# Encoder block on one Trainium2 core: the output projection as seven half-size products, its weight sums prepared during branch A, and two attention maps joined by one multiply-add

## Chip, cores, metric

One of the eight cores of a Trainium2 chip. The metric is the device time of one execution in microseconds (us); lower is better.

## What is computed

A hybrid encoder block on 1024 tokens and 16 meta tokens, width 1024, all in float32. The part that matters here:

```python
proj = rms_norm(h) @ w_in                 # q, k, v of branches A and B, and two gates
y_a  = differential_attention(...)        # branch A: 4 heads, per head two softmax maps
#        attn = softmax(s1) - lam * softmax(s2); y = attn @ v; y = rms_norm(y) * (1 - lambda_init)
y_b  = windowed_gqa(...)                  # branch B
merged = sigmoid(ga) * (y_a @ w_ba) + sigmoid(gb) * (y_b @ w_bb)
h = h + merged @ w_o                      # the output projection, 1024 x 1024 x 1024
h = h + (silu(n @ w_gate) * (n @ w_up)) @ w_down     # n = rms_norm(h), inner width 2816
out = rms_norm(h)[:, 16:]
```

## The kernel before

Every product in this kernel keeps float32 accuracy by splitting both operands into a high half (a copy rounded to the matmul's type, made by ScalarE, "ACT") and a low half (operand minus high half, a subtraction on VectorE, "DVE", or GpSimd, "POOL"), and adding three matmuls: high x high, high x low, low x high. The helper `split` (L116 to L118) issues this pair; L117 is the ACT line, L118 the subtraction's, for all tiles.

The stages in order: the input norm and the projections for branches A and B with branch B's attention (to about 330 us); branch A, 4 heads x 8 tiles of 128 queries (330 to 608 us), into which the products that compute the two gates are filled by a list of slots; the merge (622.7 to 709.8 us), 16 products of branch B and 16 of branch A, each 12 matmuls for 128 output features and 512 tokens; the output projection (709.8 to about 801 us); the first FFN products, gate and up (to 1227 us); the down projection.

The gate products, the FFN products and the down projection are already done by the seven-product scheme of Strassen and Winograd: a product of 2 x 2 blocks with seven block products instead of eight, whose operands are sums and differences of blocks and whose results are accumulated in PSUM across products. The output projection was the one large product with eight.

**Order.** TensorE's order is written out by hand from branch A to the end (`order_pe`). The other engines and the SP queue, which issues the DMAs, are ordered by a planner that simulates the program, except for a stretch of POOL before branch A and everything in the down projection. Each engine executes its queue in order, so an instruction that waits holds all behind it.

**Branch A.** `scores_a` (L789 to L818) makes the two maps m = 1 and m = 0 of a tile: three matmul groups each, a DVE reduction with the distance bias (L805), the exponential on ACT with its row sum (L810), a reciprocal (L811). The map 1 is scaled by its reciprocal and minus lambda on POOL (L813), and DVE joins the maps (L816). TensorE's transposes of the joined map (L828) come one tile later.

```python
    nc.scalar.activation(s[m][:, 0:L], s[m][:, 0:L], AF.Exp, bias=low, scale=-1.0, accum_out=dn[:, m:m + 1])
    nc.vector.reciprocal(dn[:, m:m + 1], dn[:, m:m + 1])
    if m:
        (nc.gpsimd if t % 4 in COMBINE_POOL else nc.vector).tensor_scalar(
            s[1][:, 0:L], s[1][:, 0:L], dn[:, 1:2], neglam, ALU.mult, ALU.mult)
    yield
nc.vector.scalar_tensor_tensor(s[0][:, 0:L], s[0][:, 0:L], dn[:, 0:1], s[1][:, 0:L], ALU.mult, ALU.add)
```

`normed_a` norms the result per head; what is normed is scaled by its own mean square, `EPS` added.

**The merge.** `gated` reads a gate, applies the sigmoid and runs the 12 matmuls of `branch_mm` (L786). For branch B DVE multiplies gate and product into `tb` (L1027). For branch A DVE multiplies (L1047), POOL adds `tb` (L1048), and `split` makes the merged operand `mT` for all 1024 features and tokens. The weights are read into raw tiles (`raw_tile`, five buffers of 4 KB per partition), split by `branch_w`, `WB_BUFS` deep; gates have `GT_BUFS` = 4 buffers.

```python
order_a = [(o, h) for b in range(0, DC, 4) for h in range(2) for o in range(b, b + 4)]
for n, (o, half) in enumerate(order_a):
    if o not in ws_a:
        ws_a[o] = branch_w(ypool, o, w_ba, "a")
    gt, ps, tk = gated(1, o, half, ws_a[o], ya)
    nc.vector.tensor_tensor(gt, gt, ps, ALU.mult)
    nc.gpsimd.tensor_tensor(gt, gt, tb_row(o, tk), ALU.add)
    split(mT[:, o, 0, tk], mT[:, o, 1, tk], gt, nc.vector)
    if n >= 8:
        prep_wo(0, n - 8)
```

**The projection.** `prep_wo` reads and splits blocks of `w_o` into `op_tile` (eight buffers): 8 during the merge, 8 during the projection. `out_mm` runs 24 matmuls for each of 8 token tiles and 2 column halves (L1076), four PSUM banks at a time; `out_add` adds a bank to the residual `h2` (L1081, 16 times). `norm_f` norms a token tile (ACT square L1208, POOL L122 and L123, DVE L1210), `turn_f` transposes it and, for tiles 4 to 7, makes the sums of token halves (L1239 to L1242) for the FFN's seven products.

**The FFN's start.** `product_f` runs one of the seven products for gate (i = 0) or up (i = 1); the first twelve use only operands of products 1 and 2. Tiles 5, 6, 7 are turned before the FFN products 0, 2 and 4, each followed by `split_t`, which splits the four sums at once (DVE three lows, POOL one). `prepare` keeps weight operands ahead, at most eight tiles; it includes the weight sums on DVE (L1134 to L1140).

Of the kernel before, what the change touches and what calls it, by code (L numbers as in the profile page):

```python
# [9 lines left out]
F32 = mybir.dt.float32  # L10
# [9 lines left out]
P = 128  # L20
# [18 lines left out]
COMBINE_POOL = (0, 1, 2, 3)  # L39
# [9 lines left out]
WB_BUFS = 5  # L49
# [12 lines left out]
PAD = 96  # L62
P_BUFS = 7
S_TMP = 2
# [9 lines left out]
def encoder_block(ctx: ExitStack, tc: tile.TileContext, x, meta, norm_mix, w_in, lq1, lk1, lq2, lk2,  # L74
# [241 lines left out]
    def attend_b(g, t, qb):  # L316
# [9 lines left out]
        es = small.tile([P, 4], F32, tag="bes", name=f"bes_{nm}")  # L326
# [441 lines left out]
    apool3, close_apool3 = pool("apool3")  # L768

# [3 lines left out]

    def branch_w(p, o, src, nme, raw=None):
        if raw is None:
            raw = raw_tile(f"wbr{nme}_{o}")[:, 0:512]
            load_w(raw, o, src)
        w = raw.rearrange("p (c n) -> p c n", n=P)
        wh = p.tile([P, 2, 4, P], F32R, tag="wh", name=f"wbh{nme}_{o}", bufs=WB_BUFS)
        split(wh[:, 0], wh[:, 1], w, nc.vector if nme == "a" and o >= 4 else nc.gpsimd)  # L780
        return wh
# [6 lines left out]

    def scores_a(h, t, ld, s):  # L789
# [3 lines left out]
        mn = small.tile([P, 2, 4], F32, tag="amn", name=f"amn_{nm}")  # L793
        dn = small.tile([P, 2], F32, tag="adn", name=f"adn_{nm}")
        u0 = 896 - t * P
        for m in (1, 0):
# [13 lines left out]
            nc.scalar.activation(s[m][:, 0:L], s[m][:, 0:L], AF.Exp, bias=low, scale=-1.0, accum_out=dn[:, m:m + 1])  # L810
            nc.vector.reciprocal(dn[:, m:m + 1], dn[:, m:m + 1])  # L811
            if m:
                (nc.gpsimd if t % 4 in COMBINE_POOL else nc.vector).tensor_scalar(  # L813
                    s[1][:, 0:L], s[1][:, 0:L], dn[:, 1:2], neglam, ALU.mult, ALU.mult)
            yield
        nc.vector.scalar_tensor_tensor(s[0][:, 0:L], s[0][:, 0:L], dn[:, 0:1], s[1][:, 0:L], ALU.mult, ALU.add)  # L816
# [28 lines left out]
    def normed_a(h, c, py):  # L845
# [10 lines left out]
        nc.vector.tensor_scalar(f, pst[:, 0:4], 1.0 / P, EPS, ALU.mult, ALU.add)  # L856
# [40 lines left out]
    for n in range(AH * NT + T_LAG):  # L897
# [45 lines left out]
    order_pe.__exit__(None, None, None)  # L943
    close_apool3()
# [5 lines left out]
    tb = [ypool.tile([P, 4, S], F32, name="tb"), *yb_raw]  # L950
# [13 lines left out]
    def ps_bank(name):  # L964
        return bank(psum3, "bank", name, 8)

    pad, close_pad = pool("pad", "right")
    pad.tile([P, PAD // 4], F32, name="pad")
# [8 lines left out]
    wos = {}  # L977

    def prep_wo(q, c):
# [538 lines left out]
```

## Time and profile before

| | |
|---|---|
| median of 3 runs | 1446.95 us (1446.73 to 1448.22) |
| the profiled execution's own time | 1446.43 us |
| its span, first to last instruction | 1444.6 us |
| mean granted TensorE clock | 0.997 |
| matmuls / DVE / ACT / POOL instructions | 7279 / 1624 / 1290 / 605 |
| chain that ended last: TensorE, POOL, DVE, DMA, ACT | 80%, 6%, 5%, 3%, 2% |
| of it the output projection, PE po L1076 | 6% |

The span is what the profile's times add up to; 1.8 us of the execution lie outside it. PE is TensorE's matmuls, PEld its weight loads, which overlap; SP is the queue of the DMAs. In groups, a row has line, engine, operation, out<-in, shapes and count, then busy us and mean ns of one, then the idle time of its engine before it and what ended it. In answers on one tile or line, the three numbers behind a count are the shortest, median and longest ns of one.

### The profile page before, as it was taken

The numbers are of one execution on the slowest core, as the hardware profiler recorded it, in microseconds if no ns is written. First come the engines' busy times: TensorE is split into PE (matmuls) and PEld (weight loads), VectorE is DVE, ScalarE is ACT, GpSimd is POOL, SyncE is SP. The second block draws the span as 40 slices with busy tenths as digits, with TensorE's granted clock in tenths as the row PEclk, the third lists the DMA queues.
The fourth block names the chain that finished last, engine by engine and source line by source line (L and its number), as shares of the span: only waits on it lengthen the run. The fifth ranks groups of instructions, "written<-read, shape, count | busy, mean of one in ns | idle before, by whom it ended". The sixth has DMA issues, their size and how long they took to land.

```text
span 1444.6 us, 21159 instructions
## 1 busy us (share of the span) xinstructions
PE 1423.5 (99%) x7279; PEld 1221.1 (85%) x7279; DVE 901.6 (62%) x1624; ACT 679.5 (47%) x1290; POOL 642.6 (44%) x605
## 2 busy tenths in 40 slices
PE   8999999999999999999999999999999999999997
PEld 6988989988898989888888878888888888888886
DVE  7478536637697989624614966554555553787567
ACT  6356535545665656545413643333333333444454
POOL 5589227743333333334522665544544552000444
PEclk9999999999999999999999999999999999999999
DMA  8367668995558473586602534333332333964343
GB/s 245 87 211 231 195 160 271 283 289 208 189 168 258 147 226 126 190 255 204 224 32 88 152 103 162 110 102 110 101 103 96 110 102 102 334 205 140 124 130 139
DMA packets 188891, 242.41 MB, mean 168 GB/s; under 512 B 18208, under 2 KB 115936, under 8 KB 188784
## 3 DMA queue, kind: packets, MB, share of 16 engines
q1 hardware_dynamic: 188784, 241.07, 52.5%
q8 instruction: 57, 0.93, 0.3%
q14 instruction: 50, 0.41, 0.1%
HBM read 157.45 MB, written 77.00 MB: 162 GB/s over the span
## 4 chain that ended last, share of the span: by engine, by line
PE 80%; POOL 6%; DVE 5%; issue 4%; DMA 3%; ACT 2%; SPq 0%; POOLq 0%; DVEq 0%; ACTq 0%
PE pg L1299 27%; PE pd L1393 9%; PE pg L742 7%; PE ppa L786 6%; PE po L1076 6%; PE aps L802 3%; PE pp_qb L214 3%; PE apy L841 3%; POOL oa L118 3%; PE pp_ka L214 2%; PE pp_va L214 2%; PE apt L828 2%; PE pp_qa L214 2%; PE bpt L356 1%; PE bpy L362 1%
## 5 line engine op out<-in xcount | busy, mean ns | idle before, releaser
L118 POOL TENSOR_TENSOR wop<-wf,wop 128x512 fp32r<-128x512 f32 x128 | 173.5, 1360 | 164.7 <-ACT wop L117 150.3
L1299 PE MATMUL pg<-t,wop 128*128 128x512 f32 x1056 | 242.6, 389 | 0.0
L1299 PEld LDWEIGHTS pg<-t,wop 128*128 128x128 f32 x1056 | 198.2, 188 | 41.2
L1393 PE MATMUL pd<-ob,oa 128*128 128x512 f32 x924 | 209.9, 389 | 0.4 <-POOL oa L118 0.4
L1393 PEld LDWEIGHTS pd<-ob,oa 128*128 128x128 f32 x924 | 173.3, 188 | 36.8 <-POOL oa L118 0.9
L1299 PE MATMUL pg<-b,wop 128*128 128x512 f32 x792 | 185.6, 392 | 2.3 <-DVE c L1308 2.3
L1299 PEld LDWEIGHTS pg<-b,wop 128*128 128x128 f32 x792 | 149.4, 189 | 34.2 <-issue 2.4
L742 PE MATMUL pg<-hT_hi,gop 128*128 128x512 f32 x384 | 142.9, 397 | 0.0
L118 POOL TENSOR_TENSOR oa<-ra,oa 128x512 fp32r<-128x512 f32 x33 | 44.1, 1337 | 170.0 <-ACT oa L117 168.6
L117 ACT ACTIVATE wop<-wf 128x512 fp32r<-128x512 f32 x128 | 80.2, 631 | 83.3 <-PE pg L1299 47.8
L118 POOL TENSOR_TENSOR gop<-gr,gop 128x512 fp32r<-128x512 f32 x47 | 62.0, 1321 | 105.9 <-ACT gop L117 105.9
L117 ACT ACTIVATE oa<-ra 128x512 fp32r<-128x512 f32 x77 | 48.7, 632 | 106.1 <-PE pd L1393 46.0
L810 ACT ACTIVATE as<-as,amn 128x1040 f32<-128x1040 f32 x64 | 74.5, 1165 | 47.3 <-DVE amn L805 43.2
L1134 DVE TENSOR_TENSOR s<-wf,wf 128x512 f32<-128x512 f32 x22 | 23.7, 1077 | 107.6 <-DMA wf<-in_w_ff_gate_dram 57.4
L802 PE MATMUL aps<-ak,aq 128*128 128x392 f32 (+1 forms) x384 | 90.1, 330 | 0.7 <-DVE amn L805 0.4
L1076 PE MATMUL po<-woh,mT 128*128 128x512 f32 x384 | 88.1, 390 | 0.0
L1076 PEld LDWEIGHTS po<-woh,mT 128*128 128x128 f32 x384 | 71.9, 188 | 14.8
L742 PEld LDWEIGHTS pg<-hT_hi,gop 128*128 128x128 f32 x384 | 72.7, 189 | 11.3 <-DVE gk L747 0.2
L802 PEld LDWEIGHTS aps<-ak,aq 128*128 128x128 f32 x384 | 69.6, 189 | 14.3 <-DVE amn L805 2.0
L343 POOL TENSOR_SCALAR bs<-bs,bdn 128x432 f32<-128x432 f32 (+1 forms) x64 | 41.1, 662 | 87.1 <-DVE bdn L341 74.3
L742 PE MATMUL pg<-hT_lo,gop 128*128 128x512 f32 x192 | 76.1, 396 | 0.0
L813 POOL TENSOR_SCALAR as<-as,adn,neglam 128x1040 f32<-128x1040 f32 x32 | 39.1, 1220 | 63.9 <-DVE adn L811 44.6
(289 smaller groups left out, 3105.9 us busy)
## 6 DMA issues: line engine op xcount, KB each, us to landing
ra<-aop SPq DMA_DIRECT2D x77, 256.0 KB, 2.7
wf<-in_w_ff_gate_dram SPq DMA_DIRECT2D x24, 512.0 KB, 3.8
wf<-in_w_ff_up_dram SPq DMA_DIRECT2D x24, 512.0 KB, 3.9
aop<-as SPq DMA_DIRECT2D x44, 256.0 KB, 2.1
w_c<-in_w_in_dram SPq DMA_DIRECT2D x17, 512.0 KB, 6.1
aop<-c SPq DMA_DIRECT2D x33, 256.0 KB, 2.0
ts_d<-to SPq DMA_DIRECT2D x16, 512.0 KB, 3.4
gw<-in_w_in_dram SPq DMA_DIRECT2D x32, 256.0 KB, 4.2
```

The source lines that it names most:

```text
L117: nc.scalar.activation(hi, src, AF.Copy)
L118: lo_eng.tensor_tensor(lo, src, f32(hi), ALU.subtract)
L214: nc.tensor.matmul(ps[:, :n], a[:, c, :], b[:, c, at:at + n], start=(c == 0 and i == 0), stop=(c == DC - 1 and i == 2))
L343: nc.gpsimd.tensor_scalar(st[:, r, :W], st[:, r, :W], dn[:, r:r + 1], 1.0, ALU.mult, ALU.mult)
L742: nc.tensor.matmul(ps, op[:, a, c], quad(b, *act)[:, c], start=(p in (2, 5, 1) and c == 0 and i == 0), stop=(p in (2, 3, 4) and c == 3 and ...
L786: nc.tensor.matmul(ps, w[:, a, j, :], src(j, b, tk), start=(j == 0 and n == 0), stop=(j == 3 and n == 2))
L802: nc.tensor.matmul(ps[:, :n], qs[m][:, t * P:(t + 1) * P], ks[m][:, vv, k0:k0 + n], start=(vv == 0), stop=(vv == 1))
L810: nc.scalar.activation(s[m][:, 0:L], s[m][:, 0:L], AF.Exp, bias=low, scale=-1.0, accum_out=dn[:, m:m + 1])
L841: nc.tensor.matmul(py[:, cols], v[:kp, a, k, :], at_[:kp, k, b, :], start=(k == 0 and j == 0), stop=(k == 8))
L1076: nc.tensor.matmul(ps, mT[:, c, a, t * P:(t + 1) * P], wos[q, c][:, b], start=(c == 0 and n == 0), stop=(c == DC - 1 and n == 2))
L1299: nc.tensor.matmul(ps, op[:, x, c, :], b[:, y, c, :], start=(p in (1, 2, 5) and c == 0 and n == 0), stop=(p in (4, 2, 3) and c == 3 and n ...
L1393: nc.tensor.matmul(ps[u], oa[:, a, u * P:(u + 1) * P], ob[:, b, :], start=(p in (1, 2, 5) and j == 0 and k == 0), stop=(p in (2, 3, 4) and ...
```

## The change

1. **Output projection.** The 2 x 2 blocks of tokens (X: tokens 512 to 1023, Y: 0 to 511) and features give seven products of 512 x 512 x 512, in the order 1, 5, 6, 7, 3, 2, 4. Products 1, 6, 7 and 4 accumulate in one set of four banks, 5 and 3 in another, 2 in a third. After each, DVE adds the banks to the residual of a quarter: 28 additions.
2. **Left operands.** The differences of merged blocks (`m_sum`) and all low halves are on DVE, the high halves on ACT, issued between merge products and between row blocks of the projection. POOL's additions of `tb` are now on DVE. DVE's order is by hand from the merge of branch A to the twelfth FFN product.
3. **Right operands.** Four of the seven weight operands are sums of blocks of `w_o`. `wo_ahead` makes them in branch A, in tiles 2 to 5 of each head: reads on SP, one POOL sum, a split (ACT, POOL), a write of 512 KB to DRAM. `prep_wo` reads them back ready; the other three are read and split as before.
4. **Branch B of the merge.** All of branch A's weights are split there too, into `wba`; SP's order is by hand in this loop, and at its end the FFN's first weights and gain are read. Branch A starts with tokens 512 to 1023.
5. **Maps.** Map 1 is no longer scaled on POOL. DVE joins `s1 * f + s0` with f = minus lambda x (sum of map 0) / (sum of map 1), and map 0 is left undivided; since the result is normed, `EPS` is scaled by the square of the sum of map 0.
6. **FFN start.** Token tiles 0 to 3 are turned during product 2, tiles 4 and 5 during product 4, tiles 6 and 7 before FFN products 2 and 4. The norm's last step is issued one tile later. `split_t` splits one sum at a time by a table, lows delayed. The Silu table is loaded by a dummy activation at the end of the merge. PSUM's eight banks are two tags of four. Several tiles share buffers (`WB_BUFS` 5 to 4, copies in groups of four).

```diff
@@ scores_a @@
-            nc.scalar.activation(s[m][:, 0:L], s[m][:, 0:L], AF.Exp, bias=low, scale=-1.0, accum_out=dn[:, m:m + 1])
-            nc.vector.reciprocal(dn[:, m:m + 1], dn[:, m:m + 1])
+            nc.scalar.activation(s[m][:, 0:L], s[m][:, 0:L], AF.Exp, bias=low, scale=-1.0, accum_out=sum_of[m])
             if m:
-                (nc.gpsimd if t % 4 in COMBINE_POOL else nc.vector).tensor_scalar(
-                    s[1][:, 0:L], s[1][:, 0:L], dn[:, 1:2], neglam, ALU.mult, ALU.mult)
+                nc.vector.reciprocal(dn[:, 1:2], dn[:, 1:2])
+            else:
+                nc.vector.tensor_scalar(dn[:, 0:1], dn[:, 1:2], neglam, sum_of[0], ALU.mult, ALU.mult)
             yield
-        nc.vector.scalar_tensor_tensor(s[0][:, 0:L], s[0][:, 0:L], dn[:, 0:1], s[1][:, 0:L], ALU.mult, ALU.add)
+        nc.vector.scalar_tensor_tensor(s[0][:, 0:L], s[1][:, 0:L], dn[:, 0:1], s[0][:, 0:L], ALU.mult, ALU.add)
...
@@ branch A, preparations @@
+    def wo_ahead(n):
+        c, i = divmod(n, 4)
+        p = (7, 5, 6, 3)[i]
+        tt = nc.gpsimd.tensor_tensor
+        op = vtpool.tile([P, 2, 512], F32R, tag="vt", name=f"wo_op{p}_{c}", bufs=1)
...
+        if i == 0:
+            wo_raw[:] = [block(0, c, 1)]
+        s, b = wo_raw[0], block(1, *{7: (c, 0), 5: (4 + c, 1), 6: (c, 0), 3: (4 + c, 0)}[p])
+        if i == 0:
+            s = f32(op)[:, 1]
+            tt(s, b, wo_raw[0], ALU.subtract)
...
+        split(op[:, 0], op[:, 1], s, nc.gpsimd)
+        nc.sync.dma_start(wo_d[p, c], f32(op))
...
+        if n < AH * NT and n % NT in (2, 3, 4, 5):
+            wo_ahead(n // NT * 4 + n % NT - 2)
...
@@ merge @@
+    order_sp = tc.manual_schedule(engines={mybir.EngineType.SP})
+    order_sp.__enter__()
     for o in range(DC):
+        if o < DC - 2:
+            load_b(o + 2, w_bb, "b")
+        if o == 0:
+            load_b(0, w_ba, "a")
...
+        ws_a[o] = branch_w(wba[o // 4].rearrange("p h c (k n) -> p c h k n", n=P)[:, o % 4], o, w_ba, "a")
...
+    order_dve = tc.manual_schedule(engines={mybir.EngineType.DVE})
+    order_dve.__enter__()
+    def m_high(p, c, src):
+        hi, lo = m_ops[p][:, 0, c], m_ops[p][:, 1, c]
+        nc.scalar.activation(hi, src, AF.Copy)
+        lows.append(lambda: nc.vector.tensor_tensor(lo, src, f32(hi), ALU.subtract))
...
+    def behind():
+        if last:
+            o, half, tk, gt = last.pop()
+            nc.vector.tensor_tensor(tb_row(o, tk), tb_row(o, tk), gt, ALU.add)
+            if o < 4 and half:
+                m_high(1, o, tb_row(o, tk))
+            elif not half:
+                m_sum(5 if o < 4 else 6, o % 4)
...
         gt, ps, tk = gated(1, o, half, ws_a[o], ya)
+        if n < 4:
+            split_ya(0, n, nc.gpsimd)
+        m_low()
+        behind()
         nc.vector.tensor_tensor(gt, gt, ps, ALU.mult)
-        nc.gpsimd.tensor_tensor(gt, gt, tb_row(o, tk), ALU.add)
-        split(mT[:, o, 0, tk], mT[:, o, 1, tk], gt, nc.vector)
-        if n >= 8:
-            prep_wo(0, n - 8)
...
@@ projection @@
+    for p in (1, 5, 6, 7):
...
+        for c in range(4):
+            for u in range(4):
+                out_mm(pss[u], p, u, c)
+            if p == 1 and c == 0:
+                behind()
+            prep_wo()
+            m_low()
+            work.pop(0)()
+        m_low(2)
+        for u in range(4):
+            t, q = {1: (4 + u, 0), 5: (u, 1), 6: (u, 0), 7: (u, 1)}[p]
+            out_add(pss[u], t, q)
...
+    after = {(2, 0): 0, (2, 1): 1, (2, 2): 2, (2, 3): 3, (4, 2): 4, (4, 3): 5}
+    for p in (3, 2, 4):
...
+        for u in range(4):
+            second(p, u)
+            if p == 2 or u:
+                scale_f()
+            if (p, u) in after:
+                turn_f(after[p, u], ("bankA", "bankA"))
+            if p == 2 and u:
+                for _ in range(u - u // 3):
+                    prep_wo()
...
@@ FFN start @@
-    AFTER = {0: 5, 2: 6, 4: 7}
+    SPLITS = {0: 1, 1: 1, 2: 1, 4: 2, 5: 2, 6: 2, 7: 1, 8: 2, 9: 2, 10: 2}
     for n in range(nf):
-        prepare()
-        if n in AFTER:
...
+        if n not in range(4, 8):
+            prepare()
+        if n in (2, 4):
+            turn_f(5 + n // 2)
...
         product_f(*steps[n][1])
         used[0] -= 1
+        low_of(2)
+        for _ in range(SPLITS.get(n, 0)):
+            split_t()
```

More of the change, by code (lines that the diff above doesn't have):

```diff
@@ L1220, in turn_f @@
         for b in range(2):
-            pt = four(ps_bank(f"ptn_f{t}_{b}"))
+            pt = four(ps_bank(f"ptn_f{t}_{b}", tags[b]))
             for c in range(4):
@@ L1294, in product_f @@
         if p in (1, 2, 5):
[L1295 removed]
+            u[which] = ps_bank(f"pg_{nm}_{p}", ("bankA", "bankB")[i])
         ps = u[which]
```

317 lines of the change are left out of this document (211 added, 106 removed).

## The prediction

> **What bounds the kernel now.** I read the page's busy times first, then windows by stage, the chain by time, TensorE's waits, and last the groups of the stages that the change touches.
>
> ```profile
> span 1444.6 us, 21159 instructions
> ...
> PE 1423.5 (99%) x7279; PEld 1221.1 (85%) x7279; DVE 901.6 (62%) x1624; ACT 679.5 (47%) x1290; POOL 642.6 (44%) x605
> ```
>
> TensorE is called busy 99% of the time. That share alone could hide slow issue, so the next rows are one window for each stage: start and end, length, then busy us (instructions) of PE, PEld, DVE, ACT and POOL, the granted clock, the DMA share and GB/s. The first is one stretch of branch A, the second the merge (branch products times gates), the third the output projection with its tail, the fourth the start of the FFN.
>
> ```profile
> 470.00:540.00 70.00, 69.98 (x435) 63.43 (x434) 60.24 (x172) 40.23 (x75) 26.41 (x22) 1.00 0.58 188
> 622.70:710.00 87.30, 87.30 (x387) 72.25 (x386) 43.12 (x54) 42.29 (x72) 43.03 (x31) 1.00 0.69 213
> 709.80:801.00 91.20, 91.20 (x424) 76.01 (x424) 32.57 (x42) 27.11 (x49) 25.68 (x28) 1.00 0.26 98
> 801.00:841.00 40.00, 37.71 (x170) 30.64 (x169) 37.73 (x46) 23.86 (x43) 26.37 (x19) 0.96 0.52 145
> ```
>
> In the merge and the projection TensorE never pauses and VectorE has about half its time free. At the FFN's start it is otherwise: VectorE is busy 37.73 of 40.00 us and TensorE loses 2.29. In branch A TensorE is nearly full, with VectorE at 60.24 of 70. The chain shows the pace where nothing interrupts (start, us, what):
>
> ```profile
> 622.72 87.08 PE ppa L786 x384
> 709.80 70.73 PE po L1076 x312
> ```
>
> 87.08/384 and 70.73/312 are both 0.2267 us: each matmul of 512 columns costs that, and the projection runs at the same pace as the merge. So a matmul less in the projection is worth 0.2267 us, as long as nothing becomes late. Where TensorE did wait (us, times, longest; the first row is of 320 to 630 us, the second of 801 to 841 us):
>
> ```profile
> PE apt L828 <- DVE as L816: 2.6, 2, 1.9
> ...
> PE pg L1299 <- DVE c L1308: 2.3, 2, 2.0
> ```
>
> **The change: TensorE.** The projection was 384 matmuls:
>
> ```profile
> L1076 PE MATMUL po<-woh,mT 128*128 128x512 f32 x384 | 88.1, 390 | 0.0
> ```
>
> It is now seven products, each 4 row blocks x 4 token tiles x 3 terms = 48 matmuls of the same shape, 336 in all. 48 fewer x 0.2267 = 10.9 us off an engine that does not pause there. The transposes of the normed tokens stay.
>
> **Branch A.** The map that POOL scaled by itself (the first row, 32 times) is no longer scaled. Its factor goes into the multiply-add that VectorE already does (L816), and one small product replaces one reciprocal. New are 16 preparations: each one POOL subtraction or addition and one POOL low half (priced by the second row, a POOL two-input operation of the same shape, 1294 ns in the median), one ACT high half (third row), 20 reads of 256 KB and 16 writes of 512 KB on SP.
>
> ```profile
> L813 POOL TENSOR_SCALAR as<-as,adn,neglam x32: 1207/1219/1243, 334.2 to 586.7; 128x1040 f32<-128x1040 f32 x32
> L118 POOL TENSOR_TENSOR gop<-gr,gop x47: 1272/1294/1725, 330.4 to 613.2; 128x512 fp32r<-128x512 f32 x47
> L117 ACT ACTIVATE gop<-gr x47: 612/633/639, 329.7 to 611.4; 128x512 fp32r<-128x512 f32 x47
> L816 DVE SCALAR_TENSOR_TENSOR as<-as,adn,as x32: 1279/1300/2242, 337.1 to 589.9; 128x1040 f32<-128x1040 f32 x32
> ```
>
> POOL: 32 x 1.22 = 39.0 us out, 32 x 1.29 = 41.4 us in, 2.4 more over 270 us on an engine busy 26.41 of 70: hidden. ACT: 16 x 0.63 = 10.1 us more on an engine busy 40.23 of 70: hidden, unless it lands just before an exponential. SP waits for the POOL result before each write, and the gate's reads and writes queue behind it; but gate weights are read four products ahead and a tile takes about one. Neither POOL operand nor gate read is among TensorE's waits. What can matter is the fourth row: L816 is 1.28 us when undisturbed and up to 2.24, and TensorE already waits 2.6 us for it, so its slack is small. The bounds: 2.6 us gained if those waits go; 16 x (2.242 - 1.279) = 15.4 us lost if each preparation delays one critical L816. As many POOL instructions leave as come (32 and 32), so I take 0.
>
> **Merge.** POOL's additions (16, the rows L1048) go to VectorE, which gets 8 differences besides; low halves of the merged operand stay on VectorE, 12 of them within this stage. The weights of branch A are all split on POOL during branch B.
>
> ```profile
> L1048 POOL TENSOR_TENSOR gt<-gt,tb 128x512 f32<-128x512 f32 x8 | 12.0, 1509 | 3.0 <-DVE gt L1047 3.0
> L1047 DVE TENSOR_TENSOR gt<-gt,ppa 128x512 f32<-128x512 f32 x16 | 10.8, 674 | 0.0
> ...
> L118 DVE TENSOR_TENSOR mT<-gt,mT x16: 677/1182/1778, 675.2 to 718.1; 128x512 fp32r<-128x512 f32 x16
> ```
>
> VectorE in the second half of the merge (16 products x 12 x 0.2267 = 43.5 us): 16 multiplies + 16 additions + 8 differences + 12 lows = 52 x 0.68 = 35.4 us. That fits, if each costs the 677 ns minimum. The third row says when it does not: the same instruction took 1182 ns in the median and 1778 at most, while POOL worked beside it. The Trainium skill (SBUF — State Buffer, Who interferes with whom) gives a reason: a VectorE instruction with two SBUF inputs and a GpSimd one that reads SBUF exclude each other for a whole instruction; the trace's spread agrees. By that rule every operation that moves from POOL to VectorE here is exposed, which speaks against the change; but it also takes POOL out of the way. In this stage POOL keeps only 4 lows of the branch input, so I cost the collisions at nothing; eight PSUM banks cover a lag of up to eight products.
>
> SP's order is fixed by hand through branch B: a read of weights waits for one of five raw buffers, and gates queue behind it. Typical landings:
>
> ```profile
> gt<-g_d SPq DMA_DIRECT2D x32, 256.0 KB, 3.1
> ...
> wbrb<-in_w_branch_b_dram SPq DMA_DIRECT2D x6, 256.0 KB, 6.4
> ```
>
> Weights are read two row blocks (four products, 10.9 us) ahead, gates four buffers ahead, so landings of 3.1 and 6.4 us are covered; cost 0. If the cover is gone, every us late past 10.9 is a us of TensorE.
>
> **Output stage.** VectorE: 1 addition, 8 differences, 16 lows, 28 additions into the residual (16 before), 8 normings, 10 lows and 8 sums of the turned tokens.
>
> ```profile
> L1081 DVE TENSOR_TENSOR h<-h,po 128x512 f32<-128x512 f32 x16 | 10.9, 686 | 50.2 <-PE po L1076 50.2
> L1210 DVE SCALAR_TENSOR_TENSOR xn_f<-h,rstd_f,gffn 128x1024 f32<-128x1024 f32 x8 | 10.3, 1282 | 3.3 <-POOL rstd_f L123 3.3
> L1224 PE MATMUL ptn_f<-ident,xn_f 128*128 128x128 f32 x64 | 8.0, 272 | 0.0
> L118 POOL TENSOR_TENSOR woh<-wo,woh 128x512 fp32r<-128x512 f32 x16 | 22.5, 1409 | 38.1 <-ACT woh L117 38.1
> ```
>
> 71 x 0.69 + 8 x 1.28 = 59.2 us, against 336 x 0.2267 = 76.2 us and 48 transposes x 8.0/64 = 6.0 us of TensorE: covered. Two joins are tight. (1) The seventh product accumulates in the banks of the sixth, which VectorE must read first: the first bank is complete 9 matmuls (2.0 us) before the sixth ends, and four additions of 0.69 follow while TensorE needs one bank each 3 matmuls (0.68). Nothing is lost while VectorE's queue is less than about 1.3 us behind; beyond that each us is one of TensorE. (2) The last weights of the fourth product need a raw buffer freed by a turn, then a read, ACT and POOL; 3.1 + 0.63 + 1.41 = 5.1 us against 2.7 + 1.0 + 2.0 = 5.7 us of cover. I take 0 for both, at most 3.9 each (a wait of 2.0 with the price of restarting, below).
>
> ```profile
> wo<-in_w_out_dram SPq DMA_DIRECT2D x13, 256.0 KB, 3.1
> ```
>
> **FFN start.** Now the loss there, from the timeline (start, us, engine, line, idle before):
>
> ```profile
> 817.92 13.89 PE L1299 MATMUL pg<-b,wop 128*128 128x512 f32 x60 [0.28 <-DVE c L1308]
> ...
> 833.83 7.34 PE L1299 MATMUL pg<-b,wop 128*128 128x512 f32 x24 [2.01 <-DVE c L1308]
> ...
> 835.00:840.00 5.00, 5.00 (x17) 3.95 (x16) 5.00 (x9) 2.14 (x4) 1.43 (x1) 0.70 0.14 52
> ```
>
> After 2.01 us idle, 24 matmuls took 7.34 us where 24 x 0.2267 = 5.44 are due, and the granted clock was 0.70 for 5 us. So the two waits (2.29) cost 2.29 + 1.90 = 4.2 us. The Trainium skill (TensorE: Matmul & The Clock Gate, Part 1: The HAM clock gate) says that the clock is halved after an idle window of about 3.4 us; here 2.0 us did it.
>
> The cause is the row above: VectorE full for 40 us. In the new order, token tiles 4 and 5 are turned before the FFN (5 was after), high halves and lows are spread over ten products, and the Silu table is loaded earlier. VectorE's work in the first twelve products: 10 for the two turns, 12 lows, 9 of results, 7 weight sums = 38 x 0.68 = 25.8 us, plus 1.7 carried over from the last product (4 normings + 14 others = 14.7 us in 13.0), in 12 x 2.72 + 2 x 1.0 = 34.6 us. Undisturbed that fits and 4.2 us come back. But POOL has 16 lows there, and 7 collisions at 1778 - 677 = 1.1 us use up the slack. I take half: 2.1 us.
>
> **Sum.** Against the profiled execution's own 1446.43 us (0.5 below the runs' median): 1446.43 - 10.9 - 2.1 = 1433.4.
>
> **The rivals.** (a) VectorE becomes the bound. It took over POOL's additions and the schedule by hand fixes its order from the merge to the twelfth FFN product, so a low that waits for ACT holds the residual additions behind it. For: 1182 ns in the median beside POOL, and joins with 1.3 us of slack. Against: half its time is free in the projection. Price: nothing gained at the FFN's start and both joins lost, 1446.43 - 10.9 + 2 x 3.9 = 1443.3; with one join, 1439.4.
>
> (b) Slower: the preparations in branch A. POOL's two reads each time meet L816, which has two SBUF inputs and on which TensorE's transposes wait. Price 0.96 us per call that delays a critical L816. Above 11 of the 16 the whole gain is gone; with all 16 it is 1446.43 - 10.9 + 15.4 = 1450.9. For: L816 is the one wait of TensorE there. Against: its median is 1300, near the minimum, with as many POOL instructions as there will be. The skill's rule named above would have the collisions, but not that they fall on critical ones.
>
> (c) No difference: the new waits equal what 48 matmuls give, through SP (weights late in branch B) or the joins: 1446.4.
>
> (d) Better: the FFN's start loses nothing (4.2) and the waits for L816 go (2.6): 1446.43 - 10.9 - 6.8 = 1428.7.
>
> **How the numbers follow.** Forecast, a gain of 8 to 15 us: 0.57. (a), 3 to 8: 0.18. (d), over 15: 0.07. (b), slower by over 2.9 us: 0.12. (c), within 2.9 us: 0.06. 0.2%, or 2.9 us, is about what a measurement of this kernel can tell from no change. Faster 0.57 + 0.18 + 0.07 = 0.82, same 0.06, slower 0.12. The range reaches from (d)'s end to (a)'s, 1428.7 to 1443.3, and leaves out (b) and (c).
>
> **What would show it.** 336 matmuls in the projection, unbroken at 0.2267; the chain in branch A without L813, L816's median still near 1300; VectorE's two-input operations in the merge near 680 instead of 1182; less than 2 us of TensorE's waits at the FFN's start. I am wrong if branch A is longer than before from the first gate product to the last, if TensorE waits for residual additions or weights in the projection, or if the granted clock dips there.

## The result and the profile after

| | before | after |
|---|---|---|
| median of 4 runs each, us | 1447.59 (1446.73 to 1448.81) | 1457.94 (1453.56 to 1458.41) |
| ratio to before | 1 | 1.0063 (95% interval 1.0050 to 1.0077) |
| the profiled execution | 1446.43 | 1458.41 |
| its span | 1444.6 | 1456.6 |

The change makes the kernel 10 us slower, where 13 us less were forecast. The head of the page after:

```profile
span 1456.6 us, 21178 instructions
...
PE 1420.8 (98%) x7231; PEld 1213.3 (83%) x7231; DVE 941.2 (65%) x1680; ACT 695.3 (48%) x1315; POOL 627.5 (43%) x593
```

TensorE does 48 matmuls less, which at 0.2267 us is 10.9 us, but it is busy only 2.7 us less, in a span that is 12.0 us longer. So two things were added: some 8 us in which matmuls ran slower, and 14.7 us of idle time. To find where, I took from the timelines of both kernels the start of the first matmul of each stage, and the lengths between them:

| stage, us | before | after | difference |
|---|---|---|---|
| branch A (first score matmul to merge) | 295.9 | 312.4 | +16.5 |
| merge | 87.1 | 87.1 | 0 |
| output projection to first FFN product | 92.3 | 89.3 | -3.0 |
| FFN gate and up | 425.3 | 423.3 | -2.0 |
| down projection to the end | 217.4 | 218.1 | +0.7 |

One of the eight turns (1.0 us of transposes) lies in the projection's row now and not in the FFN's. Windows of the kernel after, with the columns of the prediction; first the stretch of branch A that was shown of before, then the merge, three parts of the projection, and the FFN's first 40 us:

```profile
470.00:540.00 70.00, 64.70 (x387) 58.46 (x387) 57.26 (x158) 37.79 (x71) 19.20 (x16) 0.95 0.60 198
638.90:726.00 87.10, 87.10 (x386) 72.11 (x385) 41.95 (x64) 42.82 (x68) 28.02 (x22) 1.00 0.85 277
726.00:731.00 5.00, 2.30 (x10) 1.37 (x8) 3.02 (x6) 2.94 (x6) 0.00 (x0) 0.98 0.19 57
731.00:736.00 5.00, 3.48 (x9) 2.50 (x9) 3.61 (x6) 3.66 (x6) 0.00 (x0) 0.50 0.06 16
736.00:815.30 79.30, 78.93 (x370) 65.55 (x368) 47.43 (x67) 30.78 (x55) 20.53 (x26) 0.99 0.40 139
815.30:855.30 40.00, 38.95 (x181) 32.05 (x180) 38.51 (x46) 23.10 (x44) 23.71 (x17) 1.00 0.52 145
```

The first row was 69.98 us busy with 435 matmuls, and is 64.70 with 387. The merge is still full. The projection loses its first ten microseconds: 2.30 us busy in five, then five at half clock. The FFN's start is better than it was (38.95 of 40 against 37.71). TensorE's waits, first in branch A, then from the projection on (us, times, longest):

```profile
PE pg L738 <- DVE gk L743: 5.2, 2, 4.8
PE apt L864 <- DVE as L852: 3.6, 4, 2.0
PE aps L838 <- DVE amn L841: 2.9, 6, 1.2
...
PE po_x L1194 <- DVE gt L1171: 4.2, 2, 2.7
PE pg L1472 <- POOL wop L114: 1.0, 1, 1.0
```

**The projection's start.** Three rows of SP's queue, then TensorE (start, us, engine, line, tiles, idle before and what ended it):

```profile
677.07 1.65 SPq L1111 DMA_DIRECT2D gp<-in_w_ff_up_dram  x1
678.81 4.34 SPq L1083 DMA_DIRECT2D wo<-in_w_out_dram  x1
683.25 1.25 SPq L1062 DMA_DIRECT2D gt<-g_d  x1
...
725.95 1.52 PE L1194 MATMUL po_x<-woh,mo 128*128 128x512 f32 x6
730.17 1.12 PE L1194 MATMUL po_x<-woh,mo 128*128 128x512 f32 x3 [2.70 <-DVE gt L1171]
732.82 7.51 PE L1194 MATMUL po_x<-woh,mo 128*128 128x512 f32 x22 [1.52 <-DVE gt L1171]
```

The first gate of branch A's half of the merge is read at 683.25, behind the FFN's first weights and a read of `w_o` whose issue took 4.34 us. TensorE begins that half at 682.4 (16 x 12 matmuls of 0.2267 before 725.9), so the sigmoid and the product of gate and bank (L1171) start late and stay late: the last three read their banks at 729.44, 730.76 and 732.09, up to 6.2 us behind the end of the merge on TensorE. Two views show why VectorE does not catch up. The first has the two halves of that stretch of the merge; the second has ACT and VectorE just before the last three reads:

```profile
682.40:704.00 21.60, 21.60 (x97) 17.87 (x96) 9.06 (x15) 9.25 (x16) 6.29 (x5) 1.00 0.87 299
704.00:726.00 22.00, 22.00 (x99) 18.22 (x98) 19.71 (x32) 7.93 (x14) 0.00 (x0) 1.00 0.54 188
...
727.04 0.63 ACT L1063 ACTIVATE gt<-gt 128x512 f32<-128x512 f32 x1 [3.42 <-DMA gt<-g_d]
727.58 0.61 ACT L1126 ACTIVATE mo<-tb 128x512 fp32r<-128x512 f32 x1
...
728.23 0.69 DVE L1127 TENSOR_TENSOR mo<-tb,mo 128x512 fp32r<-128x512 f32 x1 [1.95 <-ACT mo L1126]
...
729.44 0.68 DVE L1171 TENSOR_TENSOR gt<-gt,ppa 128x512 f32<-128x512 f32 x1
```

VectorE's work for a product is four operations there, about as long as TensorE's 12 matmuls (2.72 us): it is busy 9.06 of the first 21.6 us and 19.71 of the last 22. Then a low half (L1127) waits 1.95 us for ACT, which waits for a gate's read, and by the order written by hand the product that would free a bank (L1171) stands behind it.

The kernel before had nearly the same lag. Its last product of gate and bank starts at 714.99, 5.2 us after the end of the merge at 709.8:

```profile
714.99 0.68 DVE L1047 TENSOR_TENSOR gt<-gt,ppa 128x512 f32<-128x512 f32 x1
```

It cost nothing there, because the projection could take any of eight banks. After, the first product asks for four banks of one tag, and two of them still hold results of the merge. TensorE waits 2.70 and 1.52 us, and 22 matmuls then take 7.51 us where 22 x 0.2267 = 5.0 are due.

**Branch A.** Its pace can be read off one group: the joining of the maps, 32 times, first and last start behind the durations. Before it went from 337.1 to 589.9, 252.8 us; after it takes 269.2:

```profile
L852 DVE SCALAR_TENSOR_TENSOR as<-as,adn,as x32: 1280/1301/2346, 337.2 to 606.4; 128x1040 f32<-128x1040 f32 x32
```

The largest single loss, 7.5 us, lies between the first and the second join of the third head. Timeline rows of ACT, DVE and PE there:

```profile
473.75 0.63 ACT L113 ACTIVATE wo_op<-wo 128x512 fp32r<-128x512 f32 x1 [1.57 <-DMA wo_d<-wo_op]
474.28 0.58 ACT L867 ACTIVATE at<-apt 128x512 fp32r<-128x512 f32 x1
...
474.90 0.69 DVE L868 TENSOR_TENSOR at<-apt,at 128x512 fp32r<-128x512 f32 x1 [1.77 <-ACT at L867]
...
476.35 1.30 DVE L852 SCALAR_TENSOR_TENSOR as<-as,adn,as 128x1040 f32<-128x1040 f32 x1
...
478.17 0.68 DVE L743 TENSOR_TENSOR gk<-pg,gk 128x512 f32<-128x512 f32 x1
...
479.00 0.76 PE L738 MATMUL pg<-hT_hi,gop 128*128 128x512 f32 x1 [4.79 <-DVE gk L743]
```

ACT holds a preparation's high half, which waits 1.57 us until the write of the preparation before has landed (its buffer is the same). The copy of transposed maps that VectorE needs stands behind it, and VectorE stands for 1.77 us. From 474.90 VectorE works without pause, but its gate addition (L743, 478.17) stands behind the join and other steps; TensorE waits for that addition for 4.79 us and comes back at half clock (its matmuls of 512 columns start 0.43 us apart there, not 0.2267). So the write explains at most 1.8 of the 4.79 us; the rest is the place that the planner gave the gate addition in VectorE's queue. The Trainium skill (PSUM — Partial Sum Buffer, Engine vs sequencer instructions) calls the queues of ScalarE, VectorE and GpSimd strictly first in, first out; these rows agree, with 1.77 us of VectorE behind one wait of ACT. In the whole of branch A, ACT waited for such writes and POOL for the high halves (us, times, longest):

```profile
ACT wo_op L113 <- DMA wo_d<-wo_op: 8.0, 6, 2.9
...
POOL wo_op L114 <- ACT wo_op L113: 22.5, 12, 5.7
```

The planner had also drawn all 16 preparations forward, into 340 to 488 us, the first half of branch A, where the program text spreads them over four heads.

### The profile page after: what moved, and what is told of

It is laid out like the page before. It is cut to its first block, busy times and chain, and to the rows that moved or that the text cites. A ratio compares the mean times of both kernels' runs of the same rounds, so it can differ in the third digit from the quotient of the medians.

```text
span 1456.6 us, 21178 instructions
## 1 busy us (share of the span) xinstructions
PE 1420.8 (98%) x7231; PEld 1213.3 (83%) x7231; DVE 941.2 (65%) x1680; ACT 695.3 (48%) x1315; POOL 627.5 (43%) x593
## 5 line engine op out<-in xcount | busy, mean ns | idle before, releaser
L113 ACT ACTIVATE oa<-ra 128x512 fp32r<-128x512 f32 x77 | 48.7, 632 | 107.0 <-PE pd L1588 43.8
L329 DVE CUSTOM_DVE_ANT_0 bs<-bps,tbx,nsink 128x432 f32<-128x432 f32 (+1 forms) x64 | 38.2, 623 | 38.7 <-PE bps L327 29.3
L841 DVE CUSTOM_DVE_ANT_0 as<-aps,dist,far_a 128x392 f32<-128x392 f32 x64 | 39.6, 619 | 30.5 <-PE aps L838 30.0
L877 PE MATMUL apy<-at,av 128*128 128x256 f32 x400 | 59.0, 291 | 0.0
```

The source lines that it names most:

```text
L113: nc.scalar.activation(hi, src, AF.Copy)
L329: nc.vector.tensor_tensor_reduce(st[:, r, :W], ps[:, :W], tb, 2.0 ** -(4 * g + r + 1), nsink[:, 4 * g + r:4 * g + r + 1], ALU.add, ALU.min ...
L841: nc.vector.tensor_tensor_reduce(s[m][:, k0:k0 + n], ps[:, :n], far_by, slope, low, ALU.add, ALU.min, mn[:, m, i:i + 1])
L877: nc.tensor.matmul(py[:, cols], v[:kp, a, k, :], at_[:kp, k, b, :], start=(k == 0 and j == 0), stop=(k == 8))
```

## Experiments

Each is a version of before or of after with one thing changed. Differences are of medians, to the kernel before on the same chip (1447.3 to 1448.2). "Pace" is the time from the first joined map to the last in the profiled run, 252.8 before and 269.2 after; 0.2% is 2.9 us.

**The two changes in branch A, each alone, and the two halves of one.** Theory: the preparations' waits in the queues. Rival: collisions with L852, or the joined maps. `e1_maps` puts only the new `scores_a` and `normed_a` into before; `e2_prep` only `wo_ahead` with its call (its results are not used); `e3_prep_no_dma` reads each kind of block once and writes nothing; `e4_prep_dma_only` has all reads and writes through one buffer and no sums or halves.

```diff
 e3: block():
+            if j in once:
+                return once[j]
-        nc.sync.dma_start(wo_d[p, c], f32(op))
 e4: wo_ahead():
-        tt(...); split(op[:, 0], op[:, 1], s, nc.gpsimd)
+        # every block is read into one op, which is written
```

> The kernel before with the joined maps alone; the map is no longer scaled on POOL, everything else stays. Theory (the preparations' transfers and the waits for them hold ACT and POOL in branch A): the maps cost nothing, -3 to 0 us against before. Rival (the new joining step puts VectorE's chain later): 3 to 12 us longer, with TensorE's waits for the joining multiply-add well above 2.6 us.

> The kernel before with the 16 preparations in branch A alone; their results are not used and the output projection is the old one. Theory: they carry branch A's loss, 8 to 18 us longer than before, the last gate product ending that much later than 622 us. Rival (maps): within 3 us of before.

> As e2_prep, but the blocks are read once and nothing is written: 32 POOL and 16 ACT instructions stay, 18 of 20 reads and 16 writes are left out (so the sums are of repeated blocks). Theory (waits for transfers): most of the loss goes, at most 3 us longer than before. Rival (POOL's two-input instructions exclude VectorE's, or ACT and POOL are simply too full): as slow as e2_prep within 3 us.

> As e2_prep, but without the sums and splits: 20 reads and 16 writes of raw blocks through one buffer, no POOL or ACT work. If SP's queue and the transfers themselves delay the gates' and heads' reads: 6 us or more longer. If the loss needs ACT and POOL to wait for them: 0 to 4 us. If it is the POOL work: 0.

Measured: e1 1451.84, +4.1 us (ratio 1.0032, 1.0017 to 1.0046); e2 1455.58, +7.8 (1.0053, 1.0033 to 1.0073); e3 1452.73, +5.0 (1.0043, 1.0027 to 1.0058); e4 1468.41, +20.7 (1.0152, 1.0134 to 1.0170). The joins of e1, e2 and e3, all 32 of each:

```profile
L821 DVE SCALAR_TENSOR_TENSOR as<-as,adn,as x32: 1278/1300/1834, 338.4 to 596.2; 128x1040 f32<-128x1040 f32 x32
...
L846 DVE SCALAR_TENSOR_TENSOR as<-as,adn,as x32: 1280/1301/2300, 338.6 to 599.7; 128x1040 f32<-128x1040 f32 x32
...
L847 DVE SCALAR_TENSOR_TENSOR as<-as,adn,as x32: 1280/1302/2462, 336.9 to 596.5; 128x1040 f32<-128x1040 f32 x32
```

Both changes cost by themselves: paces 257.8 and 261.1, and 5.0 + 8.3 is most of the 16.4. The forecast that the maps alone cost nothing was wrong; the preparations alone came just under their 8 to 18 us. What it is in the preparations that costs is less clear. The theory gave e3 at most 3 us, and it lost 5.0; the rival had it within 3 us of e2, which it is (2.9 less, and the two intervals overlap). So without the writes and with 2 of 20 reads most of the loss is still there.

Nor are collisions ruled out. The medians of the joins stay at 1300 ns, but a median hides a short stretch of long ones. In e3 POOL's 32 sums and low halves start between 341.6 and 422.0 us. These are the joins from 326 to 402 us, in the kernel before and in e3, then the copies that follow each join in the whole of branch A, in e1 and in after:

```profile
L816 DVE SCALAR_TENSOR_TENSOR as<-as,adn,as 128x1040 f32<-128x1040 f32 x9 | 11.7, 1297 | 0.5
...
L847 DVE SCALAR_TENSOR_TENSOR as<-as,adn,as 128x1040 f32<-128x1040 f32 x8 | 14.8, 1850 | 0.9 <-POOL as L844 0.4
...
L822 DVE COPY as<-as 128x32 f32<-128x32 f32 x32 | 8.8, 275 | 0.0
...
L853 DVE COPY as<-as 128x32 f32<-128x32 f32 x32 | 15.5, 484 | 0.0
```

Beside dense POOL work a join takes 1850 ns in the mean instead of 1297. The copies suffer too: in after 15 of 32 took over 200 ns, at most 1282 where the shortest took 148, and all 15 ran beside a POOL operation; of the 17 others 4 did. Joins and copies together take, in us:

| before | e1 | e2 | e3 | after |
|---|---|---|---|---|
| 54.5 | 50.8 | 58.6 | 61.9 | 59.3 |

So beside the joined maps alone (e1) the preparations lengthen these two steps by 8.5 us of VectorE's time in after; how much of it TensorE waited for is not shown. e3 does not separate the causes either: it has no writes to wait for, but its POOL work is denser than e2's and collides more. How the loss divides between collisions, waits for transfers and the planner's new order stays open.

e4 tells little of the change: with one buffer, reads wait for the write in SP's own queue and the gates behind them, and most is lost before the first join, which starts at 353.3 instead of 337.1. In the change the reads have buffers of their own. (Rows of e4, TensorE's wait and SP's from 320 to 420 us.)

```profile
PE pg L742 <- ACT gate_stage L750: 10.0, 2, 9.0
...
SPq L783 <- DMA wo_d<-wo_op: 21.8, 9, 7.7
```

**The projection's banks, and the preparations' place.** `e5_eight_banks` is after with all banks under one tag of eight. `e6_pinned` is after with every preparation cut into three steps (write the last and read; sum; split), one each half tile in tiles 1 to 6 of each head, and its instructions kept at their place in program order. `e7_pinned_eight_banks` is both.

```diff
 e5:
-        if tag is None:
-            tag = ("bankA", "bankB")[n_bank[0] % 2]
-            n_bank[0] += 1
-        return bank(psum3, tag, name, 4)
+        return bank(psum3, "bank", name, 8)
 e6:
+            if slot % 8 == 0 and n < AH * NT and (1 <= n % NT <= 6 or n == AH * NT - 1):
+                wo_step()          # each instruction in it under tc.keep_in_program_order
```

> The changed kernel with PSUM's eight banks under one name again, as before the change, instead of two names of four. Theory (the first product of the projection asks for all four banks of one name, two of which still hold merge products that VectorE, 8 us behind, has not read): the two waits of 4.2 us and the half clock after them go, 6 to 8 us shorter than the changed kernel, 1450 to 1452. Rival (VectorE's backlog itself is the bound): the wait moves to the next product or its additions, less than 3 us gained.

> The changed kernel with the 16 preparations issued by hand in half-tile steps through all four heads (read, sum, split, write each a step later, tiles 1 to 6 of each head), each instruction kept behind what its queue already holds; same instructions, same bytes, same buffers. Theory (waits for transfers at the head of ACT and POOL, and the planner's bunching of all 16 into the first two heads): branch A ends 8 to 16 us earlier than in the changed kernel, 1442 to 1450. Rival (collisions of POOL's and VectorE's reads, which stay as many): less than 4 us gained.

> Both edits on the changed kernel. If the two losses are separate they add: 14 to 22 us shorter than the changed kernel, 1436 to 1444, which is faster than before. If both go back to one cause (VectorE late), less than the sum.

Measured: e5 1452.31 (1.0035, 1.0021 to 1.0049), 5.6 less than after; e6 1449.91 (1.0008, 0.9993 to 1.0023), 8.0 less; e7 1445.15, 2.6 us below before (0.9990, 0.9980 to 0.9999). In e5 TensorE passes from the merge through the first three products without a pause:

```profile
715.80 8.78 PE L817 MATMUL ppa<-ya,wba_od 128*128 128x512 f32 x38
724.42 11.04 PE L1191 MATMUL po_x<-woh,mo 128*128 128x512 f32 x48
735.30 11.04 PE L1191 MATMUL po_y<-woh,mo 128*128 128x512 f32 x48
```

The stage takes 82.3 us: 92.3 - 10.9 + 1.0 for the turn is 82.4. The late gates are still there; eight banks cover them. So 7.0 us of after's loss in the profiled run (5.6 in the medians, where 6 to 8 were expected) are shown to be the division of the banks.

Pinning fell short of its theory, which had branch A end 8 to 16 us earlier: branch A goes from 312.4 to 308.4 (e6) and 306.2 (e7) in the profiled runs. Single runs differ by some 2 us there, since e5 took 310.4 with branch A's text untouched. In e6 another 3.3 us came from the projection (86.0), where TensorE's waits at its start fell from 4.2 to 1.7 us. e7 is 12.8 us below after, where 14 to 22 were expected. So the planner's place for the preparations is part of the loss, about 4 us, and some 10 us of branch A are left. Collisions explain little of these 10: joins and copies take 54.0 us in e7, against 54.5 before and 50.8 in e1.

**The joined maps: the order or the step?** Each edit of branch A makes the planner draw a new order; with joined maps 78 of VectorE's 456 places differ. `e8_maps_old_order` is e1 held in the order of before, `e9_before_new_order` is before held in e1's, by order-only edges between neighbours on DVE, ACT, POOL and SP. `e10_all_old_order` holds e7 in the order of before. `e12_maps_scaled` is e1 with POOL's scaling kept:

```diff
 e8 to e10, at the end of branch A:
+    for eng, order in ORDER.items():
...
+        for a, b in zip(order, order[1:]):
+            tc.add_manual_dep(region[b], region[a].name, ...NoSync..., reason="order")
 e12:
+                nc.gpsimd.tensor_scalar(s[1][:, 0:L], s[1][:, 0:L], dn[:, 1:2], neglam, ALU.mult, ALU.mult)
             else:
-                nc.vector.tensor_scalar(dn[:, 0:1], dn[:, 1:2], neglam, sum_of[0], ALU.mult, ALU.mult)
+                nc.vector.tensor_scalar(dn[:, 0:1], sum_of[0], ones, ones, ALU.mult, ALU.mult)
```

> The kernel before with the joined maps alone, and branch A's instructions on VectorE, ScalarE, GpSimd and SyncE held in the order in which the kernel before issues them (the scalings on GpSimd are gone, eight small products of the sums are put where the planner likes). With the joined maps alone and a free order branch A took 302.0 us instead of 295.9. If the loss lies in the order that the planner draws anew when an instruction changes (78 of VectorE's 456 places differ, 6 of ScalarE's 248, 20 of SyncE's 170): branch A 294 to 298 us and 1443 to 1448 in all. If it lies in the joined step itself: about 302 us and 1451 to 1453 in all.

> The kernel before with nothing changed but the order of branch A's instructions on VectorE, ScalarE, GpSimd and SyncE, which is that of the kernel with joined maps (the 32 scalings on GpSimd are put where the planner likes). If the order makes the loss: branch A 300 to 304 us, 1451 to 1455 in all. If the joined step makes it: branch A about 296 us and 1446 to 1449 in all.

> The whole change with preparations in half-tile steps, eight PSUM banks under one tag, and branch A's old instructions in the order of the kernel before; the preparations' own sums, splits, reads and writes stand between them in their steps. With the free order branch A took 306.2 us and the whole 1445.2. If the order makes most of what is left of the loss: branch A 296 to 301 us and 1435 to 1441 in all. If the joined step and the preparations' own work make it: branch A 304 to 307 us and 1443 to 1446 in all.

> The kernel before with the joined maps alone, but the scaling of the second map kept on GpSimd where it was, and the small step on VectorE kept at its size (it multiplies the first map's sum by ones). Free order. If branch A's loss comes from GpSimd's freedom (splits of gate weights that run earlier, reads that start earlier): branch A 296 to 298 us and 1446 to 1449 in all. If it comes from the steps on VectorE (32 small steps that are 0.11 us longer, eight more on the sums, the order around them): 300 to 303 us and 1450 to 1453 in all.

Measured: e8 1449.19, +1.0 (1.0010, 1.0001 to 1.0019); e9 1447.48, -0.7 (0.9996, 0.9987 to 1.0004); e10 1449.71, +1.5 (1.0010, 1.0000 to 1.0020); e12 1451.31, +3.6 (1.0024, 1.0015 to 1.0033). The joins of e8, e9 and e12:

```profile
L827 DVE SCALAR_TENSOR_TENSOR as<-as,adn,as x32: 1280/1301/2241, 338.9 to 595.2; 128x1040 f32<-128x1040 f32 x32
...
L822 DVE SCALAR_TENSOR_TENSOR as<-as,adn,as x32: 1280/1300/1955, 337.6 to 591.4; 128x1040 f32<-128x1040 f32 x32
...
L822 DVE SCALAR_TENSOR_TENSOR as<-as,adn,as x32: 1279/1298/2115, 336.3 to 593.5; 128x1040 f32<-128x1040 f32 x32
```

The theory that a new order costs by itself has fallen: the old kernel in the new order is not slower. Nor is it POOL's freedom, since e12, with POOL as busy as before, still loses 3.6. What is left lies with VectorE's steps. In the medians, holding the old order takes back about 3 of the 4.1 us, but the intervals of e1 and e8 just meet, and the profiled run of e8, its slowest, has branch A at 301.2 us, where e1 had 302.0. The step between the last exponential and the join takes 272 ns in place of the reciprocal's 160, 32 x 0.11 = 3.6 us. The eight products of sums are new; they take 5.6 us in e1 and 3.4 in e8. How these steps turn into lost time was not found. In e10 the old order makes branch A worse (pace 269.6): an order drawn without preparations is not one for a kernel with them.

**What is left in branch A.** `e11_old_maps_best` is e7 with the maps of before. `e13_sums_beside` takes all preparations out of branch A: maps as before, eight banks, and `prep_wo` reads the blocks and lets POOL sum and split them beside the merge and the products. `e14_sums_beside_maps` is the same with joined maps.

```diff
 e13, prep_wo, for p in (5, 6, 7, 3):
-            nc.sync.dma_start(f32(op), wo_d[p, c])
+            tt(b[0], b[0], b[1], ALU.subtract if p == 7 else ALU.add)       # tt: POOL
+            if p in (6, 3):
+                tt(b[0], b[0], b[2], ALU.subtract)
+            if p == 3:
+                tt(b[0], b[3], b[0], ALU.subtract)
+            split(op[:, 0], op[:, 1], b[0], nc.gpsimd)
```

> The whole change with preparations in half-tile steps and eight PSUM banks under one tag, but with the maps joined as in the kernel before (both reciprocals, the scaling on GpSimd). With joined maps branch A took 306.2 us and the whole 1445.2. If the joined step costs branch A here what it cost alone (some 4 to 6 us): branch A about 300 to 302 us and 1439 to 1442 in all. If GpSimd needs the room that the joined step gives it (32 scalings of some 1.3 us beside the preparations): branch A 306 us or more and 1445 or more in all.

> Seven products on eight banks under one tag, maps joined as in the kernel before, and no preparation in branch A at all: the sums of w_o blocks are made by GpSimd beside the merge and the products, where it stood still in the kernel with eight banks (44 block reads in place of the 16 prepared pairs, 28 sums more on GpSimd of about 1.3 us). Branch A's instructions are those of the kernel before. If the preparations in branch A are what is left of the loss: branch A 295 to 298 us, output projection 82 to 84 us, FFN 423, 1434 to 1438 in all. If branch A is slower from something else of the change (memory layout, the last loads): branch A 302 to 306 us and 1441 to 1446. If GpSimd's chain of sums comes late to the third and fifth product: output projection 86 to 92 us and 1439 to 1446.

> As e13_sums_beside, but with the joined maps of the change. If the joined step costs branch A what it cost alone: branch A 299 to 302 us, and 3.5 to 6 us more than e13_sums_beside. If its loss was only a matter of that kernel's order of transfers: within 1 us of e13_sums_beside.

Measured: e11 1445.12 (0.9985, 0.9972 to 0.9998); e13 1451.13 (1.0024, 1.0015 to 1.0033); e14 1454.93 (1.0057, 1.0040 to 1.0074). Joins of e7, e11 and e13:

```profile
L871 DVE SCALAR_TENSOR_TENSOR as<-as,adn,as x32: 1280/1298/2104, 337.3 to 599.9; 128x1040 f32<-128x1040 f32 x32
...
L867 DVE SCALAR_TENSOR_TENSOR as<-as,adn,as x32: 1279/1301/2245, 338.6 to 600.2; 128x1040 f32<-128x1040 f32 x32
...
L818 DVE SCALAR_TENSOR_TENSOR as<-as,adn,as x32: 1279/1302/2252, 339.3 to 593.7; 128x1040 f32<-128x1040 f32 x32
```

With the preparations gone the pace is 254.4, 1.6 from before's, and branch A is shorter by 7.5 us with the old maps (298.3 in e13, 305.8 in e11) and by 6.2 with the joined ones (300.0 in e14, 306.2 in e7). So most of the 10 us that pinning left are the preparations' being there; by which of their steps stays open. Beside them the two ways to join the maps cost the same (e7 and e11). Without them the joined maps cost 3.8 us in the medians (e14 against e13), near e1's 4.1, of which the profiled runs show 1.7 in branch A and 1.0 in the projection.

But e13 pays elsewhere: its projection takes 96.6 us instead of 82.3. The windows of 42 us in that stage, e13 first, then e7; TensorE's wait in e13; then VectorE's low halves and one of its differences in e13, and the same difference in e7 (shortest, median, longest ns):

```profile
726.00:768.00 42.00, 35.07 (x143) 28.27 (x142) 33.95 (x32) 10.90 (x20) 38.48 (x26) 0.92 0.49 151
...
732.00:774.00 42.00, 42.00 (x187) 34.79 (x186) 26.51 (x38) 9.59 (x17) 7.24 (x10) 1.00 0.43 148
...
PE po_x L1166 <- DVE h L1171: 6.9, 2, 5.4
...
L1099 DVE TENSOR_TENSOR mo<-yb_raw,mo x12: 692/1752/1842, 739.0 to 773.0; 128x512 fp32r<-128x512 f32 x12
L1114 DVE TENSOR_TENSOR tb<-tb x4: 685/1776/1795, 723.8 to 733.2; 128x512 f32<-128x512 f32 x4
...
L1158 DVE TENSOR_TENSOR tb<-tb x4: 684/686/689, 723.6 to 730.2; 128x512 f32<-128x512 f32 x4
```

With POOL busy 38.48 of 42 us, VectorE's operations on two SBUF inputs take 1.75 us in the median instead of 0.69, and the residual additions come too late for the banks (6.9 of 9.4 us of TensorE's waits in that stage). The additions themselves, which read one operand from PSUM, stay at 0.68:

```profile
L1171 DVE TENSOR_TENSOR h<-h,po_x 128x512 f32<-128x512 f32 x15 | 9.5, 678 | 3.6 <-PE po_x L1166 3.6
```

The Trainium skill (SBUF — State Buffer, Who interferes with whom) has this as a lock that is held for a whole instruction, between a VectorE operation with two SBUF inputs and a GpSimd one that reads SBUF. The rows agree, on both sides: 1.75 us is 0.69 plus most of a GpSimd operation (1.29), and the additions with one SBUF input were not slowed.

**The best version** is e7 or e11, 2.6 us below before, with intervals that just leave out no change: the seven products with eight banks and preparations in small steps at a fixed place. The gain of the products (82.2 us in the stage against 92.3) is nearly spent in branch A.

## Why the prediction was wrong

In the profiled runs the span grew by 12.0 us where 13.0 less were forecast. Of these 25 us, 16.5 are branch A's term, 8.0 the projection and the FFN's start together (-5.0 for -13.0), and 0.7 the down projection, which the forecast did not have.

- **48 matmuls fewer at 0.2267 us: right.** With eight banks the stage came to 82.3 of 82.4 us.
- **The merge: right in its length.** It takes 87.1 us as before. VectorE's low halves there went from 1182 ns in the median to 693 with POOL out of the way, so the collisions priced at nothing did cost nothing. But the sum of 35.4 us in 43.5 was an average: VectorE was busy 9.06 of the first 21.6 us and 19.71 of the last 22, and ended 6.2 us late.
- **"Eight PSUM banks cover a lag of up to eight products": the step that failed in the projection.** The diff made two tags of four of them, and the first product asks for four of one tag at once. The lag itself was priced at 0 under "gates four buffers ahead". It was 6.2 us, and 5.2 in the kernel before, where the banks covered it. Neither of the two joins that I called tight (sixth to seventh product, the last weights of the fourth) lost anything; the join that did, merge to first product, was not on my list. The price of restarting was near: 1.9 us forecast, 2.5 measured after 4.2 us idle.
- **Branch A at 0: the step that failed most.** I added busy times, found POOL and ACT with room on average, and took 0 where 16.5 us were lost. Alone, the preparations cost 7.8 us and the joined maps 4.1. Of the preparations' part, about 4 us went when they were spread and given a fixed place. Two costs are seen that the sum did not have. One is waits inside a queue: ACT 8.0 us for the writes, with a copy that VectorE needs behind one of them (the sentence on SP's writes saw the DMAs but not that the buffer's next user is ACT). The other is collisions: 8.5 us more of VectorE's time in joins and copies than in e1. How much each gave of the 16.5 us, and what the 10 us are that a fixed place left, stays open. My bound of -2.6 to +15.4 nearly held the 16.5 by luck: it was for collisions with L816, and the joins took no longer than before (43.8 us together, 44.3 before).
- **Rival (b) was right in place and sign, and in part in mechanism.** It had the preparations in branch A and 1450.9 us, 7 us short. Collisions are seen, but in the changed kernel they lengthen the copy behind the join more than the join. Judging L816 by its median of 1300 ns, as I did, cannot show them.
- **Rival (a)'s lost joins did not occur, but its mechanism did**: a low half that waits for ACT held the merge's last products behind it for 1.95 us, at the one border that was not on the list.
- **Joined maps at 0: wrong by 4 us alone.** POOL's scaling could go without a gain (e12), and the steps that were put on VectorE cost, among them eight products of sums that the sum left out.
- **The FFN's start, -2.1: half right.** TensorE's waits there fell from 2.3 to 1.9 us without the long pause at half clock, and 1.0 of the -2.0 us is the turn that moved.

By its own list, the prediction was to count as wrong if branch A was longer or if the clock dipped in the projection. Both happened.

## What to carry to other kernels

Before work is added to an engine that is half free, ask for each new instruction what it waits for and who stands behind it in its queue, and when in the stage the engine is full; a share of busy time over the stage says nothing of either. To see collisions, take the mean over the stretch where both engines work, not the median of the whole. When PSUM banks are divided into tags, count the lag of the engine that empties them against the banks of one tag, at the border between stages too. A sum that is cheap on GpSimd is not cheap beside VectorE's two-input operations: e13 moved the preparations out of branch A, which gained 7.5 us, and lost some 14 in the projection.

## What the runs showed of the hardware

- Two pauses of 2.70 and 1.52 us, 1.1 us of work apart, brought the granted clock to 0.50 for the next 5 us (window 731 to 736). The Trainium skill (TensorE: Matmul & The Clock Gate, Part 1: The HAM clock gate) gives an idle window of about 3.4 us; here the two together were 4.2 us within 5.4.
- An operation of VectorE with two SBUF inputs went from 0.69 to 1.75 us in the median while GpSimd did such operations nearly without pause, and 15 of GpSimd's 26 in those 42 us took 1.54 to 1.79 us instead of 1.29.
- In the kernel after, 15 of 32 copies of 128 x 32 elements on VectorE took over 200 ns (148 at least, 1282 at most), all 15 beside a running GpSimd operation.
- A single DMA issue on SP took 4.34 us of the queue (678.81), while the FFN's weights issued at 676.39 and 677.07 were still being read (they landed 8.7 and 9.7 us after their issue).
